# A Hymba layer on one Trainium2 core: the fourth pair's Gram blocks later, the second pair's norms later, a narrower first chunk

## The chip, the cores and the metric

One core of one Trainium2 chip runs the whole layer. The core has a matrix engine (TensorE, PE in the profile), VectorE (DVE), ScalarE (ACT), GpSimd (POOL), and SyncE (SP), which here issues most of the transfers. The metric is the device time of one execution in microseconds, lower being better.

## What is computed

The layer normalises 528 rows (16 learned tokens and 512 of the input) of 2048 features, projects them once, mixes them in two branches, and projects back. Group A is the RWKV-7 recurrence over 16 heads of 64; group B is a gated convolution of width 3.

```python
hn = _rmsnorm(h_res, norm_in_g[l])
P = hn @ w_in[l]
...
def step(S, inp):
    r_t, w_t, k_t, v_t, kk_t, b_t = inp
    sa = jnp.einsum('bhvk,bhk->bhv', S, kk_t)
    S = (S * w_t[:, :, None, :]
         - sa[..., None] * b_t[:, :, None, :]
         + v_t[..., None] * k_t[:, :, None, :])
    y_t = jnp.einsum('bhvk,bhk->bhv', S, r_t)
    return S, y_t
```

All arithmetic is float32. The output has 512 rows of 2048.

## The kernel before

**The flow.** The input projection runs as 65 column groups of 128 columns. Each float32 product is three matmuls: high half of the weights by high half of x, high by low, low by high (`steps`, L319 to L331, matmul L328). These matmuls are one long generator, here called the flow. A group is named after its columns: `ps_g` is a gate, `ps_r`, `ps_k`, `ps_v` are the operands of a head pair, `ps_B`, `ps_C`, `ps_h`, `ps_gc` belong to the convolution. A group takes two of the four accumulator banks of the pool `main`, so its first matmul must wait until whoever last used that bank has been read out.

**What stands between the flow.** All other matrix work is written by hand into the flow. `fill(ns)` lets the flow run for so many nanoseconds of planned time (0.43 ns for each moving column, so about 110 ns for 256 columns) and then returns to the code that called it; the table `FW` holds the lengths. `until(what, i)` runs the flow until a group is ready. `later(ns, fn)` issues a transfer when the flow has got so far. So a number in `FW` sets where on TensorE's queue a piece of other work stands. The order on TensorE is exactly that of the program; on the other engines a scheduler sets the order by priorities, and a block under `ahead()` is given a higher one.

**A head pair.** `prepare(i)` (L627 to L831) runs for eight pairs of heads, numbered 0 to 7. It builds decay factors (a scan into `cc`, L641), the left operand `ar`, and the right operand `bk` with three 64-column parts for each of nine chunks of 64 rows (DVE L649 and L660). ACT then copies between the two halves of the 128 partitions: L652 fills part 2 of the lower half, L661 part 2 of the upper half, L662 part 0 of the upper half. After a fill of `gram` or `gram_b` plus `shift` come the 36 Gram matmuls (L684): for each chunk and head one 64-row product of `bk` and `ar`. They write six tiles: `g_0` and `g_4` for chunks 0 to 7, and `g_8` for the last chunk, which takes two banks of `main`. DVE multiplies each by a mask into `gt` (L694); that read frees the banks. Then follow a fill of `gram2` minus `shift`, the norms (`n_misc`, `n_tz`, `zb`, L716 to L720), and on DVE two transposes of `bk` into `bt` (L730) and one of `v` into `vs` (L822). Because `shift` is added before the Gram blocks and taken off after them, a change of it moves the Gram blocks and leaves the norms where they were. Of the Gram matmuls only those of the upper half read a copied part, that of L661; what L652 and L662 write is read by L730 alone.

**Who else uses the engines.** ACT and either DVE or POOL split each new block of weights into its halves (tile `w`, L134 and L135). DVE also scales each finished group out of its banks (`pr_g`, `pr_v` and so on, L352).

**The recurrence.** `invert` solves the triangular systems of two pairs together and stores the results in a DRAM buffer `opd`. `recur` (L939 to L1025) then walks over nine chunks. `load_chunk` (L931 to L937) reads, for every pair, a slab of 128 partitions by 640 columns of `opd` into `ct`; SP issues these loads. Columns 0 to 127 of a slab hold `ar` (`O_AR`), the following ones the Gram blocks, the solved operands and `bt`. Chunk 0 starts from a zero state. So its first products `rz` (L958) are only those of the Gram part, and the products with `ar` (the branch `part == 0`, and L979 under `if c`) are left out. The recurrence begins after the fill `begin`, which follows the last `invert`.

Of the kernel before, what the change touches and what calls it, by code (L numbers as in the profile page):

```python
# [18 lines left out]
P = 128  # L19
# [6 lines left out]
NCH = SEQ // CH + 1  # L26
# [11 lines left out]
OPW = 10 * CH  # L38
O_AR, O_G, O_UV, O_B = 0, 128, 384, 512
# [2 lines left out]

FW = dict(
    evac=34, start=1062, lora=2200, gram=8000, gram_b=13500, gram2=5500, misc=2000, v=2000, vt=1000, solve=24500, solve_first=30000,
    tr=3200, lev=3000, cp=4200, out=1500, begin=20100, p=2900, u=2900, s=5200, last=3700, mix=2600,
)


# [29 lines left out]
def hymba_kernel(ctx: ExitStack, tc: tile.TileContext, xt, xtok, front, w_in, w_out, pv, lup, cst, msk, gf, out):  # L78
    nc = tc.nc
    ctx.enter_context(tc.manual_schedule(engines={mybir.EngineType.PE}))  # L80
    cp = ctx.enter_context(tc.tile_pool(name="cp", bufs=1))
# [12 lines left out]
    def col(off, i=0):  # L94
        return pvt[:, off + i : off + i + 1]
# [201 lines left out]
    with tc.issue_after(head):  # L297
        nc.vector.tensor_scalar(
            out=omm, in0=pvt[:, V_MU : V_MU + 33], scalar1=-1.0, scalar2=1.0, op0=ALU.mult, op1=ALU.add
        )  # L300
        for d, off in (
# [4 lines left out]
                out=d, in0=pvt[:, off : off + 8], scalar1=0.5, scalar2=None, op0=ALU.mult  # L306
            )
        nc.vector.tensor_scalar(
            out=hv[:, 4], in0=pvt[:, V_KA : V_KA + 8], scalar1=-0.5, scalar2=1.0, op0=ALU.mult, op1=ALU.add
# [232 lines left out]
    def step():  # L542
        t = next(flow, None)
        if t is None:
            run_pending(float("inf"))
        else:
            clock[0] += t
            run_pending(clock[0])
        return t

    def fill(ns):
        while ns > 0:
            seen = len(ready)
            t = step()
            if t is None:
                return
            ns -= t
            if len(ready) > seen:
                ns += FW["evac"]
# [26 lines left out]
    def c3(t):  # L586
        return t.rearrange("p (c s) -> p c s", s=CH)
# [10 lines left out]
    def split(t, name, n):  # L598
        hi = tr(f"{name}_h", F32R)[:, 0:n]
        lo = tr(f"{name}_l", F32R)[:, 0:n]  # L600
        nc.scalar.copy(hi, t)
        nc.vector.tensor_tensor(out=lo, in0=t, in1=hi.bitcast(F32), op=ALU.subtract)
        return hi, lo
# [6 lines left out]
    def spot(i, row, rows_n, c0, cn, step, o, n):  # L610
        d = opd[i]
        return bass.AP(
            tensor=d.tensor, offset=d.offset + (c0 * P + row) * OPW + o, ap=[[OPW, rows_n], [step * P * OPW, cn], [1, n]]
        )
# [12 lines left out]
    def prepare(i):  # L627
        p = i % 2
# [3 lines left out]
        bk = cq.tile([P, NCH, 3, CH], F32, tag="bk", name=f"bk{i}")  # L632
# [16 lines left out]
        nc.vector.scalar_tensor_tensor(  # L649
            out=bk[:, :, 1], in0=c3(k), scalar=hv[:, 2, i : i + 1], in1=c3(te), op0=ALU.mult, op1=ALU.mult  # L650
        )
        nc.scalar.copy(bk[0:64, 0 : NCH - 1, 2], bk[64:128, 0 : NCH - 1, 1])  # L652
        nc.gpsimd.tensor_scalar(
            out=ta, in0=ta, scalar1=hv[:, 3, i : i + 1], scalar2=hv[:, 4, i : i + 1], op0=ALU.mult, op1=ALU.add
        )
        nc.vector.scalar_tensor_tensor(
            out=ar[:, :, 0], in0=c3(k), scalar=col(V_KK, i), in1=e1[:, :, 0:CH], op0=ALU.mult, op1=ALU.mult
# [1 line left out]
        nc.vector.tensor_tensor(out=ta, in0=ta, in1=k, op=ALU.mult)  # L659
        nc.vector.tensor_tensor(out=bk[:, :, 0], in0=c3(ta), in1=c3(e2), op=ALU.mult)  # L660
        nc.scalar.copy(bk[64:128, :, 2], bk[64:128, :, 0])  # L661
        nc.scalar.copy(bk[64:128, 0 : NCH - 1, 0], bk[0:64, 0 : NCH - 1, 1])  # L662
        nc.gpsimd.tensor_copy(dd[:, :, place[i]], e1[:, :, CH])
        nc.gpsimd.memset(ar[:, 0, 1], 0.0)
        until("r", i)
# [2 lines left out]
            out=ar[:, 1:NCH, 1], in0=c3(r), in1=e1[:, 1:NCH, 1 : CH + 1], op=ALU.mult  # L668
        )
        nc.vector.scalar_tensor_tensor(  # L670
            out=r, in0=r, scalar=hv[:, 5, i : i + 1], in1=ta[:, CH:LP], op0=ALU.mult, op1=ALU.mult
# [3 lines left out]
        nc.scalar.activation(sq, k, AF.Square, scale=col(V_KK, i))  # L675
        sqh, sql = split(sq, f"sq{i}", LP)
        rh, rl = split(r, f"rk{i}", SEQ)
        shift = {0: 2000, 1: 2500, 3: -4000}.get(i, 0)
        fill(FW["gram_b" if p else "gram"] + shift)

        gt = cq.tile([P, 2, NCH, P], F32, tag=f"gt{p}", name=f"gt{i}")
# [9 lines left out]
        def masked(z, c0, c1):  # L691
            with ahead():
                for h in range(2):
                    nc.vector.tensor_tensor(  # L694
                        out=gt[:, h, c0:c1],
                        in0=z[h],
                        in1=gmask[:, h].unsqueeze(1).to_broadcast([P, c1 - c0, P]),
                        op=ALU.mult,
                    )
# [7 lines left out]
        masked(za, 0, 4)  # L707
        masked(zc, 4, 8)
        masked(ze, 8, 9)
        fill(FW["gram2"] - shift)  # L710

        n2 = tr(f"n2{i}")
        zn = [pool.tile([2, 288], F32, tag=t, name=f"n2_{i}_{t}") for pool, t in ((pi, "misc"), (pz, "tz"))]
# [12 lines left out]


        bt = cq.tile([P, NCH - 1, 2, CH // 2, 2], F32, tag="bt", name=f"bt{i}")
        for a in range(2):
            nc.vector.transpose(bt[:, :, :, :, a], bk[:, 0 : NCH - 1, 2 * a].rearrange("p c (t s) -> p c t s", t=2))  # L730

# [38 lines left out]
        for m in (2, 4, 8):  # L770
            for b in range(16 // (2 * m)):
# [4 lines left out]
                    out=pq,  # L776
# [5 lines left out]
                    out=tq.rearrange("p (i j) -> p i j", i=m), in_=pq, op=ALU.add, axis=AX.X  # L782
                )
                nc.vector.tensor_tensor(
                    out=pq,
# [143 lines left out]
        fill(FW["out"] if first < NPAIR - 2 else FW["begin"])  # L929

    def load_chunk(ch, c, pairs, ops):  # L931
        n = OPW if c < NCH - 1 else O_B
        if (c, 0) not in ops:
            for e in range(2):
                ops[c, e] = ch.tile([P, 4, OPW], F32, tag=f"ct{e}", name=f"ct{e}_{c}", bufs=2)
        for i in pairs:
            nc.sync.dma_start(ops[c, i % 2][:, i // 2, 0:n], spot(i, 0, P, c, 1, 1, 0, n))  # L937

    def recur(ch):  # L939
        ops = {}  # L940
        load_chunk(ch, 0, range(NPAIR), ops)
        load_chunk(ch, 1, range(NPAIR), ops)
        st = None
        pairs = [(k, e) for k in range(4) for e in range(2)]
        for c in range(NCH):
# [21 lines left out]
            if c and not last:  # L967
                load_chunk(ch, c + 1, range(4, NPAIR), ops)
# [93 lines left out]
    for i in range(0, NPAIR, 2):  # L1062
        invert([prepare(i), prepare(i + 1)])
# [9 lines left out]
    mix = [pp.tile([P, 4, SEQ], F32, tag=f"R{m}", name=f"mix{m}") for m in range(4)]  # L1073
# [256 lines left out]
    for half in range(2):  # L1330
        for g in range(4):
            b, m1, m2 = U[half, "P5", g], U[half, "M1", g], U[half, "M2", g]
# [194 lines left out]
```

## Time and profile before

| | us |
|---|---|
| median of three runs | 1004.63 |
| the three runs | 1006.38, 1004.63, 1003.05 |
| the profiled execution | 1005.19 |
| its span | 1003.4 |
| mean granted clock of TensorE | 0.997 |

The difference between the profiled execution's time and its span, 1.8 us, lies outside what the engines record. The page's lines give busy time by engine, chains of work and groups of instructions. A row of the timeline starts with the start in us and the duration in us; then come engine, line, operation and tiles, and, in brackets, how long the engine stood idle before it and for whom. Rows that follow one another with the same operation are put together ("x36"), so a row's duration then covers all of them. Ends of matmuls are modelled: two matmuls in sequence overlap, and the distance of two starts is a better measure than the duration.

### The profile page before, as it was taken

How to read it: one execution, taken by the hardware profiler on the slowest of the kernel's cores; microseconds unless marked ns; L12 is line 12 of the kernel's file. 1: busy time of each engine (PE TensorE's matmuls, PEld its weight loads, DVE VectorE, ACT ScalarE, POOL GpSimd, SP SyncE). 2: the span in 40 equal slices, each digit the busy share in tenths (PEclk: the TensorE clock that was granted, in tenths of full speed). 3: DMA queues.
4: the chain of work that ended last, by engine and by line, in shares of the span. 5: the costliest groups of instructions: out<-in, count | busy, mean ns of one | idle time of the engine just before them, and what ended most of it. 6: DMA issues, size and time to landing. Idle time of an engine off the chain costs nothing.

```text
span 1003.4 us, 22796 instructions
## 1 busy us (share of the span) xinstructions
PE 987.8 (98%) x9211; PEld 910.9 (91%) x9211; DVE 686.7 (68%) x1314; ACT 412.6 (41%) x770; POOL 266.9 (27%) x286
## 2 busy tenths in 40 slices
PE   9999999999999999999999999999999999999996
PEld 7999989999898999998999998889889898888885
DVE  6777966586765579745578745246554598999895
ACT  7554432354423435323434232232333325645553
POOL 0122323233223324232324222232323333001001
PEclk9999999999999999999999999999999999999998
DMA  9527484546673474954273954978784688798644
GB/s 324 156 79 182 113 227 105 149 135 161 152 203 97 123 189 94 240 142 111 91 204 98 235 138 109 342 270 276 227 251 136 168 256 227 241 290 224 140 103 167
DMA packets 184985, 180.00 MB, mean 179 GB/s; under 512 B 112176, under 2 KB 141616, under 8 KB 184368
## 3 DMA queue, kind: packets, MB, share of 16 engines
q1 hardware_dynamic: 182288, 169.64, 57.5%
q0 software_dynamic: 2304, 8.39, 4.8%
q8 instruction: 72, 1.18, 0.5%
q10 hardware_dynamic: 288, 0.52, 0.1%
q14 instruction: 33, 0.27, 0.1%
HBM read 139.80 MB, written 38.71 MB: 178 GB/s over the span
## 4 chain that ended last, share of the span: by engine, by line
PE 92%; DVE 3%; DMA 2%; issue 1%; ACT 1%; POOL 0%; DVEq 0%; SPq 0%; POOLq 0%
PE ps_r L328 9%; PE ps_h L328 9%; PE ps_B L328 9%; PE ps_gc L328 9%; PE ps_k L328 9%; PE ps_v L328 8%; PE ps_C L328 8%; PE M L1243 8%; PE ps_g L328 6%; PE P L1243 4%; PE Q L1243 2%; PE g L684 1%; DMA ct<-opd 1%; PE ps_lora L328 1%; PE rz L958 1%; PE zs L1005 1%
## 5 line engine op out<-in xcount | busy, mean ns | idle before, releaser
L135 POOL TENSOR_TENSOR w<-wr,w 128x512 fp32r<-128x512 f32 x119 | 169.1, 1421 | 371.7 <-ACT w L134 317.6
L134 ACT CAST w<-wr 128x512 fp32r<-128x512 f32 x252 | 153.6, 619 | 266.1 <-PE ps_k L328 44.3
L135 DVE TENSOR_TENSOR w<-wr,w 128x512 fp32r<-128x512 f32 x133 | 97.3, 736 | 107.8 <-ACT w L134 107.2
L328 PE MATMUL ps_k<-xh,w 128*128 128x256 f32 (+1 forms) x512 | 95.9, 285 | 0.2
L328 PE MATMUL ps_r<-xh,w 128*128 128x256 f32 (+1 forms) x512 | 95.2, 282 | 0.0
L328 PE MATMUL ps_v<-xh,w 128*128 128x272 f32 (+1 forms) x512 | 95.1, 283 | 0.0
L328 PE MATMUL ps_h<-xh,w 128*128 128x258 f32 (+1 forms) x512 | 93.2, 281 | 0.0
L328 PE MATMUL ps_C<-xh,w 128*128 128x258 f32 (+1 forms) x512 | 93.1, 281 | 0.0
L328 PE MATMUL ps_g<-xh,w 128*128 128x258 f32 (+1 forms) x512 | 91.6, 280 | 0.0
L328 PE MATMUL ps_B<-xh,w 128*128 128x512 f32 x256 | 83.6, 395 | 0.0
L328 PE MATMUL ps_gc<-xh,w 128*128 128x512 f32 x256 | 81.5, 392 | 0.0
L328 PEld LDWEIGHTS ps_k<-xh,w 128*128 128x128 f32 x512 | 80.1, 189 | 0.8 <-DVE w L135 0.3
L328 PEld LDWEIGHTS ps_r<-xh,w 128*128 128x128 f32 x512 | 80.3, 189 | 0.3
L328 PEld LDWEIGHTS ps_v<-xh,w 128*128 128x128 f32 x512 | 80.1, 189 | 0.3
L328 PEld LDWEIGHTS ps_C<-xh,w 128*128 128x128 f32 x512 | 79.5, 189 | 0.6
L328 PEld LDWEIGHTS ps_h<-xh,w 128*128 128x128 f32 x512 | 79.5, 189 | 0.4
L328 PEld LDWEIGHTS ps_g<-xh,w 128*128 128x128 f32 x512 | 79.2, 189 | 0.2
L328 PE MATMUL ps_k<-xl,w 128*128 128x256 f32 (+1 forms) x256 | 72.8, 284 | 0.0
L328 PE MATMUL ps_v<-xl,w 128*128 128x256 f32 (+1 forms) x256 | 72.5, 283 | 0.0
L328 PE MATMUL ps_g<-xl,w 128*128 128x256 f32 (+1 forms) x256 | 72.4, 283 | 0.0
L328 PE MATMUL ps_r<-xl,w 128*128 128x256 f32 (+1 forms) x256 | 72.2, 282 | 0.0
L328 PE MATMUL ps_h<-xl,w 128*128 128x256 f32 (+1 forms) x256 | 72.2, 282 | 0.0
(312 smaller groups left out, 2197.4 us busy)
## 6 DMA issues: line engine op xcount, KB each, us to landing
wr<-in_w_in_dram SPq DMA_DIRECT2D x126, 512.0 KB
ct<-opd SPq DMA_DIRECT2D x64, 320.0 KB
wo<-in_w_out_dram SPq DMA_DIRECT2D x21, 512.0 KB
opd<-gt SPq DMA_DIRECT2D x16, 576.0 KB
x<-in_w_out_dram POOLq DMA_DIRECT2D x16, 512.0 KB, 5.6
opd<-ar SPq DMA_DIRECT2D x8, 576.0 KB
opd<-bt SPq DMA_DIRECT2D x64, 64.0 KB
x<-in_w_out_dram SPq DMA_DIRECT2D x8, 512.0 KB
```

Source lines behind the costliest of these rows:

```text
L134: nc.scalar.copy(hi, rq)
L135: low[q] = eng.tensor_tensor(out=lo, in0=rq, in1=hi.bitcast(F32), op=ALU.subtract).ins
L328: nc.tensor.matmul(ps[r], ww[:, w], xx[:, kt, a:b], start=(kt == 0 and n == 0), stop=(kt == KT - 1 and n == 2))
L684: nc.tensor.matmul(z[h][:, c - c0], bk[hs, c, h : h + 2, :].rearrange("p a s -> p (a s)"), ar[hs, c].rearrange("p a s -> p (a s)"), start= ...
L958: nc.tensor.matmul(z[e][ho if e else hs, 0, k], ct[e][hs, k, o : o + CH], uv(e, k, hs, h) if part else st[hs, 4 * e + k], start=(part == 0 ...
L1005: nc.tensor.matmul(zs[hs, j], bb[:, h], uv(e, k, everything, h), start=True, stop=True)
L1243: nc.tensor.matmul(bank[s], left(prod, jj, m, s), w, start=(jj == 0 and n == 0), stop=(jj == 7 and n == 2))
```

## The change

Five edits. (1) The copies L652 and L662 stand later in the program text, after the norms and just ahead of the transposes that read them. Lines between L652 and L729 therefore have a number lower by one or two in the changed kernel (the Gram matmul is L682 there, the masks L692, the norms L714 to L718). (2) `load_chunk` reads for chunk 0 the columns from `O_G` on, which is 128, instead of from 0: 512 of 640 columns. (3) `begin` grows from 20100 to 20600. (4) `shift` of pair 3 goes from −4000 to −2000. (5) The fill between Gram blocks and norms of pair 1 grows by 700.

```diff
-    tr=3200, lev=3000, cp=4200, out=1500, begin=20100, p=2900, u=2900, s=5200, last=3700, mix=2600,
+    tr=3200, lev=3000, cp=4200, out=1500, begin=20600, p=2900, u=2900, s=5200, last=3700, mix=2600,
...
-        nc.scalar.copy(bk[0:64, 0 : NCH - 1, 2], bk[64:128, 0 : NCH - 1, 1])
...
-        nc.scalar.copy(bk[64:128, 0 : NCH - 1, 0], bk[0:64, 0 : NCH - 1, 1])
...
-        shift = {0: 2000, 1: 2500, 3: -4000}.get(i, 0)
+        shift = {0: 2000, 1: 2500, 3: -2000}.get(i, 0)
...
-        fill(FW["gram2"] - shift)
+        fill(FW["gram2"] - shift + 700 * (i == 1))
...
         bt = cq.tile([P, NCH - 1, 2, CH // 2, 2], F32, tag="bt", name=f"bt{i}")
+        nc.scalar.copy(bk[0:64, 0 : NCH - 1, 2], bk[64:128, 0 : NCH - 1, 1])
+        nc.scalar.copy(bk[64:128, 0 : NCH - 1, 0], bk[0:64, 0 : NCH - 1, 1])
...
-        n = OPW if c < NCH - 1 else O_B
+        a, b = 0 if c else O_G, OPW if c < NCH - 1 else O_B
...
-            nc.sync.dma_start(ops[c, i % 2][:, i // 2, 0:n], spot(i, 0, P, c, 1, 1, 0, n))
+            nc.sync.dma_start(ops[c, i % 2][:, i // 2, a:b], spot(i, 0, P, c, 1, 1, a, b - a))
```

On TensorE the same instructions run in both kernels. In pair 1 there are 34 matmuls of the flow between the Gram blocks and the norms, where there were 28. Everything of pairs 2 and 3 then stands 6 or 7 matmuls later in the flow. In pair 3 the Gram blocks stand after 80 matmuls of the group `ps_g`, where they stood after 55. The first products of the recurrence stand after 18 matmuls of the group `ps_h`, where they stood after 13.

Three places show how the instructions move. The first is the end of pair 3's Gram blocks, on TensorE and on DVE. On TensorE, 41 matmuls of the same group follow the last Gram matmul in the kernel before, and then the next group `ps_g` starts in new banks. In the changed kernel the last twelve rows up to that start are these (two matmuls, one row, stand between the last Gram matmul and the first row here; `ps_g_0_3377` and `ps_g_1_3378` are the old group's banks, `ps_g_0_3540` is the first one of the next group):

```order
L328 MATMUL ps_g_0_3377<-xl,w_3192 128x256
L328 MATMUL ps_g_0_3377<-xh,w_3192 128x256
L328 MATMUL ps_g_1_3378<-xh,w_3192 128x258
L328 MATMUL ps_g_1_3378<-xl,w_3192 128x258
L328 MATMUL ps_g_1_3378<-xh,w_3192 128x258 x2
L328 MATMUL ps_g_1_3378<-xl,w_3192 128x258
L328 MATMUL ps_g_1_3378<-xh,w_3192 128x258 x2
L328 MATMUL ps_g_1_3378<-xl,w_3192 128x258
L328 MATMUL ps_g_1_3378<-xh,w_3192 128x258 x2
L328 MATMUL ps_g_1_3378<-xl,w_3192 128x258
L328 MATMUL ps_g_1_3378<-xh,w_3192 128x258
L328 MATMUL ps_g_0_3540<-xh,w_3229 128x256
```

So 16 matmuls instead of 41 now stand between the Gram blocks and a group that starts in the bank of `g_8_0`.

On DVE, around the masks of the same pair, before:

```order
L730 STREAM_TRANSPOSE bt_3635<-bk_3138 128x512
L135 TENSOR_TENSOR w_3373<-wr_3371,w_3373 128x512
L363 SCALAR_TENSOR_TENSOR v_3359<-pr_v_3361,omm,sh_v_3367 128x16
L363 SCALAR_TENSOR_TENSOR v_3359<-pr_v_3361,omm,sh_v_3367 128x512
L730 STREAM_TRANSPOSE bt_3635<-bk_3138 128x512
L694 TENSOR_TENSOR gt_3450<-g_0_0_3451,cs 128x512
L694 TENSOR_TENSOR gt_3450<-g_0_1_3452,cs 128x512
L694 TENSOR_TENSOR gt_3450<-g_4_0_3453,cs 128x512
L694 TENSOR_TENSOR gt_3450<-g_8_0_3455,cs 128x128
L694 TENSOR_TENSOR gt_3450<-g_4_1_3454,cs 128x512
L694 TENSOR_TENSOR gt_3450<-g_8_1_3456,cs 128x128
L822 STREAM_TRANSPOSE vs_3707<-v_3359 128x576
```

The same place in the changed kernel:

```order
L730 STREAM_TRANSPOSE bt_3640<-bk_3145 128x512 x2
L135 TENSOR_TENSOR w_3371<-wr_3369,w_3371 128x512
L363 SCALAR_TENSOR_TENSOR v_3357<-pr_v_3359,omm,sh_v_3365 128x16
L363 SCALAR_TENSOR_TENSOR v_3357<-pr_v_3359,omm,sh_v_3365 128x512
L595 TENSOR_TENSOR lul_4455<-lur_4453,luh_4454 128x256
L135 TENSOR_TENSOR w_3407<-wr_3405,w_3407 128x512
L692 TENSOR_TENSOR gt_3474<-g_0_0_3475,cs 128x512
L692 TENSOR_TENSOR gt_3474<-g_0_1_3476,cs 128x512
L822 STREAM_TRANSPOSE vs_3714<-v_3357 128x576
L692 TENSOR_TENSOR gt_3474<-g_4_0_3477,cs 128x512
L692 TENSOR_TENSOR gt_3474<-g_8_0_3479,cs 128x128
```

One more split of weights (`w_3407`) stands ahead of the masks, the transpose `vs` stands in the middle of them, and a piece of the next pair's preparation (`lul`, L595) stands just ahead of them; the latter stood some 20 instructions earlier before.

The second place is SP's queue at the loads of chunk 0 (tiles `ct_0`). Before, and then in the changed kernel, up to the first load of chunk 1:

```order
L142 DMA wr_8281<-in_w_in_dram 128x1024
L937 DMA ct_0_8308<-opd_68 128x640
L451 DMA mixd_96<-cv_7887 128x512
L937 DMA ct_0_8309<-opd_69 128x640
L937 DMA ct_0_8308<-opd_70 128x640
```

```order
L142 DMA wr_8281<-in_w_in_dram 128x1024
L937 DMA ct_0_8313<-opd_68 128x512
L451 DMA mixd_96<-cv_7887 128x512
L937 DMA ct_0_8314<-opd_69 128x512
L937 DMA ct_0_8313<-opd_70 128x512
```

The order is the same and all eight loads of chunk 0 are narrower; those of chunk 1 behind them keep 640 columns. Further on, two loads of the later stage (`rb`, `gg`) stand ahead of the loads of chunk 2, where they stood behind them.

The third is DVE's queue in chunk 8, the last of the recurrence, where L988 copies what the products `zy` wait for. Before, and then in the changed kernel:

```order
L429 SCALAR_TENSOR_TENSOR cv_10292<-u_10040,pvt,cv_10292 128x512
L988 COPY ct_8_9849<-rz_0_10183 64x4x64 x2
L429 SCALAR_TENSOR_TENSOR cv_10292<-u_10040,pvt,cv_10292 128x512
L135 TENSOR_TENSOR w_10298<-wr_10296,w_10298 128x512
L1036 TENSOR_TENSOR ya_10283<-zy_10286,ya_10283 128x512
```

```order
L429 SCALAR_TENSOR_TENSOR cv_10252<-u_10040,pvt,cv_10252 128x512 x2
L988 COPY ct_8_9853<-rz_0_10187 64x4x64 x2
L135 TENSOR_TENSOR w_10258<-wr_10256,w_10258 128x512
L1036 TENSOR_TENSOR ya_10303<-zy_10306,ya_10303 128x512
L1037 TENSOR_REDUCE nv_10349<-ya_10303 128x8
```

Both convolution steps L429 now stand ahead of the two copies.

## The prediction

> **What bounds the kernel now.** I read the page first, for the engine that sets the end, and then the waits of that engine, since only time in which it stands idle can be won without taking work away. The rows of the page:
>
> ```profile
> span 1003.4 us, 22796 instructions
> PE 987.8 (98%) x9211; PEld 910.9 (91%) x9211; DVE 686.7 (68%) x1314; ACT 412.6 (41%) x770; POOL 266.9 (27%) x286
> PE 92%; DVE 3%; DMA 2%; issue 1%; ACT 1%; POOL 0%; DVEq 0%; SPq 0%; POOLq 0%
> ```
>
> TensorE is busy for 987.8 of 1003.4 us, so it stands idle for 15.6. The change removes no matmul; it can act through these 15.6 us, or make new ones. The view of TensorE's waits, and windows of 50 us (the first pair of numbers is the window's length and TensorE's busy time), say what they are and where:
>
> ```profile
> PE n_misc L716 <- DVE gt L694: 1.7, 1, 1.7
> PE rz L958 <- DMA ct<-opd: 1.4, 3, 0.5
> PE g L684 <- DVE pr_v L352: 1.1, 1, 1.1
> PE g L684 <- DVE bk L660: 0.6, 1, 0.6
> 100.00:150.00 50.00, 48.08 (x420) 47.14 (x419) 40.38 (x90) 19.57 (x36) 15.41 (x17) 1.00 0.67 169
> 250.00:300.00 50.00, 48.13 (x409) 46.77 (x408) 34.66 (x82) 15.89 (x28) 13.63 (x14) 1.00 0.67 171
> 600.00:650.00 50.00, 48.57 (x532) 43.36 (x522) 20.05 (x40) 13.65 (x26) 10.74 (x9) 1.00 0.67 219
> ```
>
> Three stages hold a gap each: 1.9 us near 130 us (norms of pair 1 wait for the masks), 1.9 us near 255 us (Gram blocks of pair 3 wait for `bk` and then for `pr_v`), 1.4 us near 636 us (the recurrence waits for its loads). The edits (5), (4) and (2) with (3) move just these three places. What is won there reaches the end only if TensorE doesn't wait again behind it; with 92% of the chain on TensorE, I take it that it arrives in full.
>
> **Edit (5), norms of pair 1 six matmuls later.** The timeline of that place:
>
> ```profile
> 125.46 0.38 PE L328 MATMUL ps_g<-xl,w 128*128 128x256 f32 x1
> 127.04 1.30 POOL L135 TENSOR_TENSOR w<-wr,w 128x512 fp32r<-128x512 f32 x1 [4.59 <-ACT w L134]
> 127.27 1.61 DVE L135 TENSOR_TENSOR w<-wr,w 128x512 fp32r<-128x512 f32 x1
> 128.74 0.28 PE L328 MATMUL ps_g<-xl,w 128*128 128x256 f32 x1
> 128.81 2.87 DVE L694 TENSOR_TENSOR gt<-g,cs 128x512 f32<-128x512 f32 x6
> 130.74 0.29 PE L716 MATMUL n_misc<-sq_h,ones 128*2 128x288 f32 x1 [1.72 <-DVE gt L694]
> ```
>
> The 28 matmuls from 125.46 to 128.74 start (128.74 − 125.46)/27 = 0.121 us apart. Six more fill 6 × 0.121 = 0.7 us of the 1.72 us in which TensorE waits for DVE. DVE's masks don't depend on these six, so they end when they did, and 1.0 us of wait stays: **−0.7**. Bounds: 0, if DVE comes later by as much; −0.7.
>
> The price is that pairs 2 and 3 stand six or seven matmuls later against groups that don't move. In pair 2 the group `ps_r` starts in the bank that the mask of `g_8` frees:
>
> ```profile
> 218.30 2.87 DVE L694 TENSOR_TENSOR gt<-g,cs 128x512 f32<-128x512 f32 x6
> 221.50 0.28 PE L328 MATMUL ps_r<-xh,w 128*128 128x256 f32 x1
> ```
>
> The fourth of the six masks is that of `g_8_0`; with four large and two small ones in 2.87 us, about 0.63 and 0.18, it ends at 218.30 + 3 × 0.63 + 0.18 = 220.4 (an estimate). That is 1.1 us ahead of `ps_r`. Seven matmuls less take 0.85 of it, and one split of weights that moves ahead of the masks takes some 0.65 more. So a wait of 0 to 0.5 us is born there; I count 0.3 for it inside the next step, where TensorE and DVE meet again.
>
> **Edit (4), Gram blocks of pair 3 twenty-five matmuls later.** TensorE and DVE there:
>
> ```profile
> 253.61 0.46 PE L684 MATMUL g<-ar,bk 64*128 64x128 f32 x2 [0.62 <-DVE bk L660]
> 254.22 2.06 PE L684 MATMUL g<-ar,bk 64*128 64x128 f32 x32 [0.15 <-ACT bk L661]
> 257.38 0.46 PE L684 MATMUL g<-ar,bk 64*128 64x128 f32 x2 [1.10 <-DVE pr_v L352]
> 257.76 0.39 PE L328 MATMUL ps_g<-xl,w 128*128 128x256 f32 x1
> 262.59 0.40 PE L328 MATMUL ps_g<-xh,w 128*128 128x258 f32 x2
> 239.93 1.36 DVE L641 TENSOR_TENSOR_SCAN cc<-smask,tz 128x576 f32<-128x576 f32 x1 [1.01 <-POOL tz L639]
> 259.78 2.84 DVE L694 TENSOR_TENSOR gt<-g,cs 128x512 f32<-128x512 f32 x6
> 262.54 0.76 DVE L822 STREAM_TRANSPOSE vs<-v 128x576 f32<-128x576 f32 x1
> 263.23 0.65 DVE L135 TENSOR_TENSOR w<-wr,w 128x512 fp32r<-128x512 f32 x1
> ```
>
> In pair 1 the 36 Gram matmuls ran unhindered (none of the waits above is theirs). Here the stage takes 257.76 − 253.61 + 0.62 = 4.8 us. Unhindered it would be the 2.06 us of 32 matmuls × 36/32 = 2.3 at most, so 2.5 to 2.6 us are lost; the waits give only 1.9, since the pipeline also drains and fills around each. 25 matmuls × 0.121 = 3.0 us put off the start by more than that, so `bk` and `pr_v` are ready and these waits go: −2.6 on their own.
>
> What is late next is the mask of `g_8_0`. Before, the next group starts with the second matmul of the row at 262.59, at 262.71, and the mask ended at about 259.78 + 3 × 0.62 + 0.18 = 261.8, so 0.9 us were to spare. Now 16 instead of 41 matmuls lie between. Without any wait that group would start at 262.71 − 2.6 − 0.7 + 0.3 = 259.7. When does DVE free the bank? Its queue from the scan `cc` to the first mask took 259.78 − 239.93 = 19.85 us, nearly all of it work in order, and the change adds one split of weights (0.65, the row at 263.23) to it, less some of the time in which it waited: 19.6 to 20.3. The transpose `vs` (0.76, some 0.7 of it not overlapped) now stands between the masks: three large masks, one small one and `vs` make 3 × 0.62 + 0.18 + 0.70 = 2.7. The bank is free 22.3 to 23.0 us after `cc` starts. `cc` itself moves forward with the flow, by 0.4, and by up to 1.0 more if POOL, for which it waited 1.01, is sooner done: 238.5 to 239.9. Free at 260.8 to 262.9, middle 261.7. This mask, not the flow, decides when the group starts: a new wait of about 2.0 us. Against 262.71 the whole of pairs 1 to 3 leaves **−1.0** (bounds −3.0, had the bank been free in time, and +0.2).
>
> The Trainium skill, in "SBUF — State Buffer", section "Who interferes with whom", says that a DVE operation with two inputs from SBUF can't run beside a GpSimd operation that reads SBUF, and that the later one is blocked for the whole of the other. The trace agrees: DVE's split at 127.27 began under POOL's and took 1.61 us, where the one at 263.23 took 0.65. By that rule the additional split could cost DVE 1.6 instead of 0.65, and the bank would come 1.0 us later; the sum would be −2.0 instead of −3.0.
>
> **Edit (1), the copies.** In the scheduled order ACT's copies keep their places in six of eight pairs and move a little in two, and no matmul waits on either in any pair. Cost **0**: ACT works 41% of the span, which hides 2 × 0.62 us per pair wherever they stand; uncovered, 1.2 us per pair only if the transposes `bt` were waited for, which the waits don't show.
>
> **Edits (2) and (3), the recurrence's start.** The first stage of chunk 0, the next stage of the same chunk for comparison, the loads in the chain of waits, and the DMA rate (the last number of the window, GB/s):
>
> ```profile
> 634.66 0.56 PE L958 MATMUL rz<-ct 64*64 64x64 f32 x20
> 637.32 0.33 PE L958 MATMUL rz<-ct 64*64 64x64 f32 x4 [0.51 <-DMA ct<-opd]
> 637.58 0.39 PE L328 MATMUL ps_h<-xl,w 128*128 128x258 f32 x1
> 640.98 0.69 PE L973 MATMUL rz<-pn,ct 64*64 64x64 f32 x32
> 641.60 0.39 PE L328 MATMUL ps_h<-xl,w 128*128 128x258 f32 x1
> 630.90 6.38 DMA ct<-opd
> 630.00:632.00 2.00, 2.00 (x19) 2.00 (x18) 0.83 (x2) 0.62 (x1) 0.00 (x0) 1.00 1.04 410
> ```
>
> The 32 matmuls of `rz` take 637.58 − 634.66 = 2.9 us, the 32 of the next stage 641.60 − 640.98 = 0.6: 2.3 are lost. The last four start at 637.32 where 635.2 would do, so the last load is 2.1 us late. The DMA engines are saturated at 410 GB/s, so bytes set the landings: eight loads lose 8 × 128 × 128 × 4 = 0.52 MB, which at 410 GB/s is 1.3 us. Five matmuls more of the flow (5 × 0.121) put the need 0.6 us later. Together 1.9 of 2.1; a wait of 0.2 stays: **−2.1**. Bounds: −2.3 (all gone), and −0.6 if a load costs the same whatever its width.
>
> The page "DMA: Bandwidth & Descriptors" of the Trainium skill, section "Bandwidth", speaks against narrower loads: it finds a higher rate for larger ones and asks for 1 MiB. No run here shows loads of two widths in this place; by its fixed part of 2.0 us ("Anatomy of one DMA — SWDGE (gpsimd) path") a load would be shortened by 5% rather than 20%.
>
> **Chunk 8.** The products `zy` wait for the copies L988:
>
> ```profile
> 776.70 1.01 DVE L429 SCALAR_TENSOR_TENSOR cv<-u,pvt,cv 128x512 f32<-128x512 f32 x1 [2.17 <-ACT cv L427]
> 777.74 0.88 DVE L988 COPY ct<-rz 64x256 f32<-64x256 f32 x2
> 778.54 0.73 DVE L429 SCALAR_TENSOR_TENSOR cv<-u,pvt,cv 128x512 f32<-128x512 f32 x1
> 778.41 1.29 PE L1009 MATMUL zy<-ct 128*64 128x64 f32 x32
> ```
>
> The second L429 now goes ahead and delays the copies by up to 0.73; TensorE, which had next to no margin (the first copy ends about 778.18, `zy` starts at 778.41), comes 0.6 later by edit (3). So 0 to 0.7; I take **+0.1**.
>
> **The sum.** −1.0 − 2.1 + 0.1 + 0 = −3.0 us. The profiled execution took 1005.19 (span 1003.4 and 1.8 around it) and becomes 1002.2; it lies 0.56 above the median, so on the scale of the median 1004.63 − 3.0 = 1001.6.
>
> **The rivals.**
> (a) The masks come in time. `cc` is at 238.5 and the queue short by a wait or two; the bank is free near 260 and the first three terms stand in full: −3.0 − 2.1 + 0.1 = −5.0, so 999.6. For it: 1.01 us of DVE's wait at `cc` can vanish. Against: even 238.5 + 22.3 is 260.8.
> (b) The new mask wait eats all of pairs 1 to 3. The bank comes at 262.7 or later, for instance with a split held up as at 127.27: 0 − 2.1 + 0.1 = −2.0, so 1002.6. For it: the row at 127.27. Against: POOL and DVE overlap only at some splits.
> (c) The loads don't shorten, since latency rather than bytes sets them (6.38 us of one load in the chain): −1.0 − 0.6 + 0.1 = −1.5, so 1003.1. Against: 410 GB/s.
> (d) Slower. The recurrence, five matmuls later in the flow, puts its copies behind the convolution's work on DVE not in chunk 8 alone but in all eight chunks from 1 on. Each time one or both of the L429 steps stand ahead, 0.73 to 1.74 us; at 0.9 that is 8 × 0.9 = +7.2, and with the other terms at −3.1 the kernel comes out +4.1, at 1008.7. It turns slower than before from 3.1/8 = 0.4 us a chunk, and by over 3.0 us from 0.8. For it: next to no margin in chunk 8. Against: in the order of instructions only chunk 8 shows such a swap.
>
> **How the numbers follow.** What a measurement of this kernel can tell from no change is about 0.3%, or 3.0 us. My forecast has a chance of 0.52; its own range is −4.3 to −1.7 and a little over half of it, 0.28, lies beyond −3.0. (a) has 0.26, as `cc` and the queue each have slack that I could only bound. (b) 0.06, (c) 0.05, (d) 0.11, with whatever else the scheduler's new order may cost. Faster: 0.28 + 0.26 = 0.54; within: 0.24 + 0.06 + 0.05 = 0.35; slower: 0.11. The range leaves out (d) and the far ends of (a): from 1004.63 − 6.0 = 998.6 to 1004.63 + 0.4 = 1005.0.
>
> **What would show it.** The wait of `n_misc` at pair 1 falls to 1.0; no wait of L682 in pair 3; a new wait of `ps_g` for DVE's masks near 259 to 262 us, about 2 us; `rz` of chunk 0 in 0.6 to 0.9 us, its loads landing some 0.66 us apart; at most 0.7 before `zy` in chunk 8. The prediction is wrong if that new wait is missing, if `rz` still takes over 2 us, or if a wait appears at a place not named here.

## The result, and the profile after

| | before | changed |
|---|---|---|
| median of seven runs, us | 1004.54 | 1009.02 |
| lowest and highest | 1003.05, 1006.38 | 1007.41, 1011.22 |
| profiled execution, its span | 1005.19, 1003.4 | 1007.93, 1006.1 |

The ratio of the changed kernel to the one before is 1.0045, with a 95% interval of 1.0031 to 1.0060: the change costs about 4.5 us. The forecast was a gain of 3.0. The two profiled executions differ by less, 1007.93 − 1005.19 = 2.7 us, since that of before lies 0.65 us above its kernel's median and that of the changed kernel 1.1 below. TensorE's waits in the changed kernel (total, times, longest, in us; the warm-up's 1.4 and 0.2 at `zb`, the same in both kernels, are left out):

```profile
PE ps_g L328 <- DVE gt L692: 5.5, 1, 5.5
PE n_misc L714 <- DVE gt L692: 1.0, 1, 1.0
PE ps_r L328 <- DVE gt L692: 0.4, 1, 0.4
PE g L682 <- DVE bk L659: 0.2, 1, 0.2
PE g L682 <- ACT bk L660: 0.2, 1, 0.2
```

Four of the five rows are what was forecast in kind and size: 1.0 us is left of the wait at the norms of pair 1, 0.4 is born in pair 2, the waits of the Gram blocks in pair 3 have nearly gone, and no wait of `rz` is left. The first row was forecast in kind, at 2.0 us. It is 5.5. Windows of five microseconds around it show a second loss (the third number from the right is the granted clock of TensorE):

```profile
255.00:260.00 5.00, 4.75 (x52) 4.24 (x52) 4.93 (x11) 4.00 (x8) 1.36 (x2) 1.00 0.52 123
260.00:265.00 5.00, 0.00 (x0) 0.00 (x0) 5.00 (x7) 0.61 (x1) 1.58 (x2) 0.71 0.79 212
265.00:270.00 5.00, 4.65 (x25) 4.65 (x26) 3.27 (x9) 1.35 (x2) 0.16 (x1) 0.61 0.77 156
270.00:275.00 5.00, 5.00 (x43) 4.74 (x41) 0.69 (x1) 2.35 (x5) 1.29 (x1) 1.00 0.00 0
```

TensorE does nothing from 260 to 265 us while DVE (the third busy time) works throughout. The clock falls, and it stays low after the work has come back: 0.71 and 0.61 in two windows are 2 × 5 × (0.29 + 0.39) = 6.8 us at half clock. The wait's other side is DVE's and POOL's timeline in the same kernel:

```profile
239.58 1.36 DVE L641 TENSOR_TENSOR_SCAN cc<-smask,tz 128x576 f32<-128x576 f32 x1 [0.62 <-POOL tz L639]
252.91 1.85 DVE L659 TENSOR_TENSOR bk<-ta,e 128x576 f32<-128x576 f32 x1
258.71 1.92 DVE L363 SCALAR_TENSOR_TENSOR v<-pr_v,omm,sh_v 128x16 f32<-128x16 f32 x2
260.89 1.75 DVE L135 TENSOR_TENSOR w<-wr,w 128x512 fp32r<-128x512 f32 x1
262.56 1.28 DVE L692 TENSOR_TENSOR gt<-g,cs 128x512 f32<-128x512 f32 x2
264.45 1.64 DVE L692 TENSOR_TENSOR gt<-g,cs 128x512 f32<-128x512 f32 x4
247.96 3.58 POOL L652 TENSOR_SCALAR ta<-ta,hv 128x576 f32<-128x576 f32 x1 [2.79 <-DVE te L648]
252.57 1.58 POOL L135 TENSOR_TENSOR w<-wr,w 128x512 fp32r<-128x512 f32 x1
258.64 1.30 POOL L135 TENSOR_TENSOR w<-wr,w 128x512 fp32r<-128x512 f32 x1 [4.49 <-ACT w L134]
260.69 1.40 POOL L135 TENSOR_TENSOR w<-wr,w 128x512 fp32r<-128x512 f32 x1 [0.51 <-ACT w L134]
265.35 0.58 PE L328 MATMUL ps_g<-xh,w 128*128 128x256 f32 x1 [5.45 <-DVE gt L692]
```

The same `bk` and `v`, and POOL's splits near them, in the kernel before:

```profile
252.72 0.75 DVE L660 TENSOR_TENSOR bk<-ta,e 128x576 f32<-128x576 f32 x1
258.35 0.88 DVE L363 SCALAR_TENSOR_TENSOR v<-pr_v,omm,sh_v 128x16 f32<-128x16 f32 x2
254.90 1.64 POOL L135 TENSOR_TENSOR w<-wr,w 128x512 fp32r<-128x512 f32 x1 [4.08 <-ACT w L134]
258.59 1.80 POOL L135 TENSOR_TENSOR w<-wr,w 128x512 fp32r<-128x512 f32 x1 [2.06 <-ACT w L134]
```

Three DVE operations take 1.75 to 1.92 us where their like took 0.75, 0.88 and 0.65 in the kernel before (the row of `v` covers two instructions each time). Each begins 0.07 to 0.34 us behind a split of weights on POOL. In the kernel before `v` overlaps with a split too, but there DVE began first, by 0.24 us: DVE took 0.88 us and POOL's split 1.80 instead of 1.30. So it matters here which of the two begins first. From the scan to the first mask it is 262.56 − 239.58 = 23.0 us instead of the 19.6 to 20.3 forecast. The scan itself starts at 239.58, which is 240.1 on the time scale of the profile before (the changed kernel's profile runs 0.5 us early, see below): 0.2 us behind the forecast range of 238.5 to 239.9.

Where did the time go? Both kernels run the flow's matmuls in the same order, so the start of the same matmul can be compared in the two traces. The table is worked out from these starts, with the difference set to zero at 60 us (the two executions began 0.5 us apart).

| behind | changed minus before, us | step |
|---|---|---|
| norms of pair 1 (140) | −0.8 | −0.8 |
| solve of pairs 0 and 1 (190) | −1.4 | −0.6 |
| masks of pair 2 (229) | −0.7 | +0.7 |
| masks of pair 3 (275) | +4.9 | +5.6 |
| solve of pairs 2 and 3 (340) | +4.8 | −0.1 |
| start of the recurrence (645) | +2.75 | −2.1 |
| chunk 8 (800) | +3.1 | +0.3 |

Pair 1 and the recurrence stand as forecast, the first solve is better by 0.6 us, and pair 2 (+0.7 for 0.3) and chunk 8 (+0.3 for +0.1) are a little worse. Pair 3 is the loss.

### The profile page after: what moved, and what is told of

Its sections match the earlier page's. It is cut to its first block, busy times and chain, and to the rows that moved or that the text cites. A ratio compares the mean times of both kernels' runs of the same rounds, so it can differ in the third digit from the quotient of the medians.

```text
span 1006.1 us, 22797 instructions
## 1 busy us (share of the span) xinstructions
PE 989.1 (98%) x9211; PEld 912.4 (91%) x9211; DVE 688.9 (68%) x1314; ACT 412.1 (41%) x770; POOL 268.9 (27%) x286
## 4 chain that ended last, share of the span: by engine, by line
PE 88%; DVE 6%; POOL 2%; issue 2%; DMA 1%; ACT 1%; DVEq 0%; SPq 0%; POOLq 0%; ACTq 0%
PE ps_C L328 9%; PE ps_gc L328 9%; PE ps_h L328 9%; PE ps_B L328 8%; PE ps_k L328 8%; PE ps_r L328 8%; PE M L1243 8%; PE ps_v L328 7%; PE ps_g L328 6%; PE P L1243 4%; PE Q L1243 2%; PE ps_lora L328 1%; PE g L682 1%; PE zs L1005 1%; PE rz L958 1%
## 5 line engine op out<-in xcount | busy, mean ns | idle before, releaser
L328 PE MATMUL ps_C<-xl,w 128*128 128x256 f32 (+1 forms) x256 | 72.5, 283 | 0.0
```

The source lines that it names most:

```text
L328: nc.tensor.matmul(ps[r], ww[:, w], xx[:, kt, a:b], start=(kt == 0 and n == 0), stop=(kt == KT - 1 and n == 2))
```

## The experiments

Each kernel was timed in five rounds beside the kernel before. E2 to E4 and E7 to E8, and E10 to E12, start from the kernel before; E1, E5, E6 and E9 from the changed kernel. The medians of the kernel before, timed beside them, are 1004.32 us for e1 to e4, 1004.42 for e5 to e8 and 1004.68 for e9 to e12; the ratio is not the quotient of the medians.

| run | median, us | ratio to before (95%) |
|---|---|---|
| e1 changed, without edit 4 | 1006.11 | 1.0018 (1.0009 to 1.0027) |
| e2 edit 4 alone | 1006.31 | 1.0023 (1.0010 to 1.0035) |
| e3 edits 2 and 3 alone | 1002.98 | 0.9994 (0.9985 to 1.0004) |
| e4 edit 5 alone | 1006.94 | 1.0032 (1.0021 to 1.0044) |
| e5 changed, three splits off POOL | 1007.25 | 1.0030 (1.0019 to 1.0041) |
| e6 changed, masks of `g_8` first | 1008.30 | 1.0038 (1.0023 to 1.0052) |
| e7 edits 2, 3, and 5 taken back | 1001.21 | 0.9977 (0.9965 to 0.9990) |
| e8 as e7, shift −3400 | 1001.52 | 0.9973 (0.9962 to 0.9983) |
| e9 changed, three other splits off POOL | 1006.36 | 1.0020 (1.0009 to 1.0031) |
| e10 edit 1 alone | 1004.64 | 1.0002 (0.9993 to 1.0011) |
| e11 edit 2 alone | 1002.45 | 0.9986 (0.9976 to 0.9996) |
| e12 as e7, with 1500 | 1001.58 | 0.9969 (0.9956 to 0.9983) |

### Which edit loses: e1 to e4

E1 puts one number back:

```diff
-        shift = {0: 2000, 1: 2500, 3: -2000}.get(i, 0)
+        shift = {0: 2000, 1: 2500, 3: -4000}.get(i, 0)
```

> The changed kernel with the shift of pair 3 back at -4000 (edits 1, 2, 3 and 5 stay). Theory A (the loss is edit 4's: the next group waits for the mask of g_8_0 at the end of a long DVE queue, and the idle time slows TensorE's clock): the wait of 5.5 us for the masks near 260 us is gone, the two waits of before for bk and pr_v are back (about 1.9 us), the clock stays at 1.00; against before: pair 1 -0.7, solve of pairs 0 and 1 -0.6, pair 2 +0.7, recurrence -2.2, chunk 8 +0.3, sum -2.5, ratio about 0.9975. Theory B (the loss is made by edit 5, which puts pairs 2 and 3 six or seven matmuls later): a wait for the masks of 3 us or more stays, ratio 1.002 or more.

Neither theory holds. The wait for the masks is gone, yet the kernel is slower than before. Its longest waits at 1.0 us and more behind the start, and the window of five microseconds in which the first of them ends (the third number from the right is the granted clock):

```profile
PE g L682 <- DVE bk L659: 2.9, 1, 2.9
PE n_misc L714 <- DVE gt L692: 1.0, 1, 1.0
...
255.00:260.00 5.00, 3.83 (x34) 3.67 (x35) 4.93 (x11) 3.67 (x6) 0.51 (x2) 0.66 0.53 123
```

The Gram blocks wait 2.9 us for `bk`, where they waited 0.6 before, and the clock is at half speed for 3.4 us of that window, 0.66 on average. So edit 5 does harm, as theory B had it, but at `bk` and not at the masks.

E2 is that line alone on the kernel before:

```diff
-        shift = {0: 2000, 1: 2500, 3: -4000}.get(i, 0)
+        shift = {0: 2000, 1: 2500, 3: -2000}.get(i, 0)
```

> The kernel before with the shift of pair 3 at -2000 and nothing else (edit 4 alone). Theory A: the next group waits 3 to 5.5 us for the mask of g_8_0, the granted clock falls to about 0.5 for some us, the waits for bk and pr_v are gone; +2.5 to +6 us against before, ratio 1.0025 to 1.006. Theory B: no wait of over 1 us, -2.6 to 0 us, ratio 0.9974 to 1.000.

```profile
PE ps_g L328 <- DVE gt L694: 1.8, 1, 1.8
PE rz L958 <- DMA ct<-opd: 1.0, 2, 0.5
```

Edit 4 alone moves the wait to the masks, as theory A said, with a period of half clock behind it. The wait is 1.8 us, not 3 to 5.5, and the ratio, 1.0023, lies just below the range given. Compared matmul by matmul, pair 3 comes 1.0 us later than in the profile of before. From `cc` to the first mask it is 258.49 − 237.52 = 21.0 us here: the 19.85 of before and the added split of weights, which took 1.15 us beside POOL.

E3 takes edits 2 and 3 alone:

```diff
-    ... begin=20100, ...
+    ... begin=20600, ...
...
-        n = OPW if c < NCH - 1 else O_B
+        a, b = 0 if c else O_G, OPW if c < NCH - 1 else O_B
```

> The kernel before with edits 2 and 3 alone (chunk 0 loads 512 of 640 columns, begin 20600). Both theories: no wait of rz for its loads, the 32 matmuls of rz in 0.6 to 0.9 us, -2.2 us, ratio about 0.9978. A third one (a later recurrence loses on DVE in every chunk) expects new waits in the chunks and a ratio of 1.000 or more.

The stage does what was expected; these are the 32 matmuls of `rz` in one piece:

```profile
634.81 0.82 PE L958 MATMUL rz<-ct 64*64 64x64 f32 x32
```

Compared matmul by matmul, the flow gains 2.2 us there against the profile of before. The ratio, 0.9994, shows less than the −2.2 us, and its interval doesn't reach 0.9978. In this profile the unchanged wait of 1.7 us at pair 1 is followed by half clock, which it is not in the profile of before:

```profile
130.00:132.00 2.00, 1.22 (x6) 0.74 (x7) 2.00 (x5) 0.68 (x2) 0.00 (x0) 1.00 0.04 8
132.00:134.00 2.00, 2.00 (x12) 1.99 (x11) 1.24 (x3) 0.59 (x1) 0.14 (x1) 0.57 0.36 78
134.00:136.00 2.00, 2.00 (x12) 2.00 (x12) 0.49 (x2) 1.13 (x2) 0.44 (x1) 0.57 0.74 128
136.00:138.00 2.00, 2.00 (x19) 2.00 (x18) 0.00 (x0) 0.11 (x1) 0.85 (x1) 1.00 0.83 209
```

That cost 1.5 us of this execution. The runs that were only timed have no trace, but their mean granted clock is on record, and it doesn't order e3's times (1004.02 us at 0.998, 1002.36 at 0.995), so half clock alone doesn't explain them. The medians, 1002.98 beside 1004.32, show a gain of 1.3 us. The gap between −2.2 and the ratio stays open.

E4 takes edit 5 alone.

```diff
-        fill(FW["gram2"] - shift)
+        fill(FW["gram2"] - shift + 700 * (i == 1))
```

> The kernel before with edit 5 alone (norms of pair 1 six matmuls later). Theory A: the wait of n_misc falls from 1.7 to 1.0 us, a wait of ps_r for the masks of pair 2 of about 0.4 us is born, and pair 3 keeps its waits; -1.3 to 0 us, ratio 0.9987 to 1.000. Theory B: the next group of pair 3 waits for the masks by 2 us or more, ratio 1.002 or more.

Slower by 0.3%, through a wait that neither theory named: `bk` in pair 3.

```profile
247.10 1.06 DVE L775 TENSOR_TENSOR prod<-d,y 72x512 f32<-72x512 f32 x1
248.08 0.75 DVE L648 SCALAR_TENSOR_TENSOR te<-ta,e 128x576 f32<-128x576 f32 x1
248.93 3.58 POOL L653 TENSOR_SCALAR ta<-ta,hv 128x576 f32<-128x576 f32 x1 [2.79 <-DVE te L648]
253.54 1.55 POOL L135 TENSOR_TENSOR w<-wr,w 128x512 fp32r<-128x512 f32 x1
253.89 1.82 DVE L660 TENSOR_TENSOR bk<-ta,e 128x576 f32<-128x576 f32 x1
255.85 0.46 PE L684 MATMUL g<-ar,bk 64*128 64x128 f32 x2 [2.32 <-DVE bk L660]
```

In the kernel before:

```profile
246.56 0.74 DVE L648 SCALAR_TENSOR_TENSOR te<-ta,e 128x576 f32<-128x576 f32 x1
248.08 1.05 DVE L775 TENSOR_TENSOR prod<-d,y 72x512 f32<-72x512 f32 x1
247.40 2.36 POOL L653 TENSOR_SCALAR ta<-ta,hv 128x576 f32<-128x576 f32 x1 [1.23 <-DVE te L648]
```

There `te` (L648) came ahead of the 512-wide step of another pair's solve (L775); now it comes behind it. `te` releases POOL's L653, which takes 3.58 us instead of 2.36. DVE's two-input operations beside it are the likely reason, but no run takes them away. POOL's next split starts 0.35 us ahead of `bk`, and `bk` takes 1.82 us. From the start of `cc` (240.55) to the start of `bk` it is 13.3 us here and 12.8 in e2, e3, e7 and the kernel before.

### What makes the mask late: e5, e6 and e9

E5 leaves out what POOL reads in three blocks (`q` counts half blocks of weights); the low halves of these weights are zero.

```diff
+        if q in (83, 85, 87):
+            low[q] = eng.memset(lo.bitcast(F32), 0.0).ins
+        else:
             low[q] = eng.tensor_tensor(out=lo, in0=rq, in1=hi.bitcast(F32), op=ALU.subtract).ins
```

> The changed kernel, with the low half of three blocks of weights left out: GpSimd's three splits of weights that run near 253, 259 and 261 us are replaced by a memset of zeros, which writes but reads nothing. The order on VectorE is the same as in the changed kernel. Theory C (the masks are late because VectorE's operations with two inputs in SBUF stand still while GpSimd's split reads SBUF): bk L659, v L363 and w L135 fall from 1.85, 1.92 and 1.75 us to about 0.75, 0.9 and 0.65, the wait for the masks from 5.5 to 2.3 to 3 us, the half clock lasts for one period of 3.4 us or none; 3 to 5 us less than the changed kernel, so ratio 0.9995 to 1.0015 against before. Theory D (VectorE's queue is simply too long; GpSimd has no part in it): those three keep their durations, the wait stays above 5 us, ratio 1.003 to 1.006.

The three blocks were those beside `v` and `w` and a later one; the split beside `bk` was still there and serves as a control. DVE in this kernel, and the memset beside `w`:

```profile
253.80 1.84 DVE L662 TENSOR_TENSOR bk<-ta,e 128x576 f32<-128x576 f32 x1
259.59 0.89 DVE L366 SCALAR_TENSOR_TENSOR v<-pr_v,omm,sh_v 128x16 f32<-128x16 f32 x2
260.73 0.69 DVE L138 TENSOR_TENSOR w<-wr,w 128x512 fp32r<-128x512 f32 x1
260.89 0.53 POOL L136 MEMSET w<- 128x512 f32 x1 [0.28 <-PE ps_g L331]
```

The two operations without a reading neighbour on POOL fall from 1.92 to 0.89 and from 1.75 to 0.69 us; the one whose neighbour stayed keeps 1.84. So theory C holds for the durations. The wait falls to 3.4 us, not to 2.3 to 3, the half clock still lasts two periods instead of one or none, and the ratio, 1.0030, misses the 0.9995 to 1.0015 expected. E9 replaces the three that stand beside `bk`, `v` and `w`:

```diff
-        if q in (83, 85, 87):
+        if q in (81, 83, 85):
```

> As e5, but with the memset in the place of those three splits of GpSimd that stood beside bk L659, v L363 and w L135 in the changed kernel (in e5 the one beside bk was still there and the third replaced one came later). The low halves of three blocks of weights are left out. Theory C: bk L659 now takes 0.75 instead of 1.85 us too, and the time from the scan cc to the first mask falls from 23.0 to about 19.8 us; the wait of the next group falls from 3.4 us in e5 to 2.0 to 2.6, with one period of half clock or none; ratio 1.000 to 1.002. Theory D: cc to the first mask stays above 21 us, ratio 1.003 or more.

```profile
239.65 1.36 DVE L644 TENSOR_TENSOR_SCAN cc<-smask,tz 128x576 f32<-128x576 f32 x1 [0.62 <-POOL tz L642]
253.00 0.75 DVE L662 TENSOR_TENSOR bk<-ta,e 128x576 f32<-128x576 f32 x1
252.61 1.00 POOL L136 MEMSET w<- 128x512 f32 x2
259.44 1.29 DVE L695 TENSOR_TENSOR gt<-g,cs 128x512 f32<-128x512 f32 x2
```

Beside a memset `bk` is back at 0.75, and `cc` to the first mask at 259.44 − 239.65 = 19.8 us, which was the forecast. So the 3.2 us by which DVE's queue was longer than forecast are the three collisions. A wait of 3.1 us stays all the same, above the 2.0 to 2.6 expected, because the flow, not held up at `bk`, wants the bank sooner. Even without collisions edits 4 and 5 together lose.

E6 puts the masks of `g_8` first:

```diff
-        masked(za, 0, 4)
-        masked(zc, 4, 8)
-        masked(ze, 8, 9)
+        if i == 3:
+            first = masked(ze, 8, 9)
+            with tc.issue_after(first):
+                masked(za, 0, 4)
+                masked(zc, 4, 8)
+        else:
+            masked(za, 0, 4)
+            masked(zc, 4, 8)
+            masked(ze, 8, 9)
```

> The changed kernel with the two masks of g_8 ahead of the other four in pair 3. All theories in which the next group waits for the mask of g_8_0 and nothing else: the wait falls from 5.5 by two large masks, to 3.3 to 3.8 us, and with it the half clock from two periods of 3.4 us to one; 1.9 to 3.6 us less than the changed kernel, ratio 1.001 to 1.0026 against before. If the group waits for something else, the ratio stays at 1.0045.

The wait falls to 3.7 us and the half clock to one period, as expected; in the profile the stage loses 1.9 us less than in the changed kernel. The ratio, 1.0038, lies above the 1.001 to 1.0026 expected and is not told apart from 1.0045.

### Edit 5 without its side effect: e7, e8 and e12

E7 takes the 700 off again in the next fill of the same pair, so that pair 2 and all behind it stand where they stood; edits 2 and 3 are in.

```diff
-        fill(FW["gram2"] - shift)
+        fill(FW["gram2"] - shift + 700 * (i == 1))
...
-        fill(FW["misc"])
+        fill(FW["misc"] - 700 * (i == 1))
```

> The kernel before with edits 2 and 3, and with edit 5 whose 700 is taken off again from the next fill of the same pair, so that pairs 2 and 3 stay where they were. Theory E (edit 5 loses because it moves pairs 2 and 3, which changes VectorE's order there): the wait of n_misc falls to 1.0 us, no wait in pair 2, pair 3 waits as before (about 1.9 us in all, no more), rz without waits; -0.7 - 2.2 = -2.9 us, ratio about 0.9971. If the later norms themselves do harm, the ratio is 1.000 or more.

Faster than before, at 0.9977. Around pair 3 DVE runs its instructions in the same order as in e3, and no wait for `bk` exists:

```profile
PE n_misc L716 <- DVE gt L694: 1.0, 1, 1.0
PE g L684 <- DVE pr_v L352: 0.6, 1, 0.6
```

So the later norms do no harm. What they push along with them does.

E8 is e7 with

```diff
-        shift = {0: 2000, 1: 2500, 3: -4000}.get(i, 0)
+        shift = {0: 2000, 1: 2500, 3: -3400}.get(i, 0)
```

> As e7, and the shift of pair 3 at -3400, half a microsecond later than before. Theory E with the mask queue as the next limit: the wait for bk (0.6 us) is gone, that for pr_v halves, the next group comes 0 to 1 us earlier until it meets the mask of g_8_0; -2.7 to -3.9 us, ratio 0.9961 to 0.9973. If any move of the Gram blocks loses, the ratio is above that of e7.

With the Gram blocks half a microsecond later, the wait for `pr_v` is gone and 0.2 us of the mask's wait appear: the two limits lie that close together. The ratio, 0.9973, is not told apart from e7's.

E12 is e7 with

```diff
-        fill(FW["gram2"] - shift + 700 * (i == 1))
+        fill(FW["gram2"] - shift + 1500 * (i == 1))
...
-        fill(FW["misc"] - 700 * (i == 1))
+        fill(FW["misc"] - 1500 * (i == 1))
```

> As e7 with 1500 instead of 700 (norms of pair 1 thirteen or fourteen matmuls later, taken back in the next fill of the pair). If the masks' end decides when the norms run: the wait of n_misc falls from 1.0 to 0.2 us or less and the rest stays; e7 less 0.8 us, ratio 0.9965 to 0.997. If the solve behind the norms becomes late: a new wait near 165 to 180 us or an order on VectorE as in e4, ratio above 0.998.

```profile
PE pwarm L187 <- DVE cold L184: 1.4, 1, 1.4
PE g L684 <- DVE pr_v L352: 0.7, 1, 0.7
PE zb L719 <- ACT n L723: 0.2, 1, 0.2
```

No wait is left at pair 1, and no new one appears: behind TensorE's warm-up (`pwarm`) that for `pr_v` in pair 3, 0.7 us, is the only one above 0.2. 0.9969 is the lowest ratio of all, though its interval overlaps with those of e7 and e8. All three are faster than both kernels.

### Edits 1 and 2 alone: e10 and e11

E10 moves the two copies as the change does; e11 takes the lines of `load_chunk`, with `begin` at 20100.

```diff
-        nc.scalar.copy(bk[0:64, 0 : NCH - 1, 2], bk[64:128, 0 : NCH - 1, 1])
...
-        nc.scalar.copy(bk[64:128, 0 : NCH - 1, 0], bk[0:64, 0 : NCH - 1, 1])
...
         bt = cq.tile([P, NCH - 1, 2, CH // 2, 2], F32, tag="bt", name=f"bt{i}")
+        nc.scalar.copy(bk[0:64, 0 : NCH - 1, 2], bk[64:128, 0 : NCH - 1, 1])
+        nc.scalar.copy(bk[64:128, 0 : NCH - 1, 0], bk[0:64, 0 : NCH - 1, 1])
```

> The kernel before with edit 1 alone (the copies later in the text). Prediction: cost 0, ratio 0.999 to 1.001, no new wait of TensorE. A rival: the new order of pairs 2 and 3 on VectorE and ScalarE, not the six matmuls, makes bk late; then the wait for bk in pair 3 is above 2 us and the ratio 1.002 or more.

1.0002 (0.9993 to 1.0011), and no new wait: edit 1 costs nothing and brings nothing.

> The kernel before with edit 2 alone (512 of 640 columns in chunk 0, begin at 20100). By bytes: the last load comes 1.3 us earlier, a lateness of 0.8 us stays of 2.1, rz in about 1.4 us instead of 2.9; -1.3 us, ratio about 0.9987. By a fixed cost for each load: rz stays at 2.5 to 2.9 us, ratio 1.000.

```profile
632.75 0.85 PE L958 MATMUL rz<-ct 64*64 64x64 f32 x28
633.94 0.33 PE L958 MATMUL rz<-ct 64*64 64x64 f32 x4 [0.35 <-DMA ct<-opd]
```

One wait of 0.35 us is left for the last load, where three made 1.4 us. The flow gains 1.5 us there and the kernel 0.9986, against −1.3 and 0.9987 expected. So the narrower load does most of the work, by its bytes, and `begin` the remainder.

## Why the prediction was wrong

**The recurrence's start: right.** −2.1 was forecast, −2.1 measured, with the split between bytes and later start confirmed by e11.

**Edit 1: right,** by e10.

**Pair 1, pair 2 and chunk 8: right in the trace, to 0.4 us.** −0.8 for −0.7 at pair 1; a wait of 0.4 for 0.3 in pair 2, which comes 0.7 later with it; and +0.3 for +0.1 in chunk 8. The 0.6 us gained in the first solve were not forecast.

**Pair 3: the step that failed.** The step read: DVE's "queue from the scan `cc` to the first mask took 259.78 − 239.93 = 19.85 us, nearly all of it work in order, and the change adds one split of weights". The mechanism was the right one. The term was mis-sized at three points.

First, 19.6 to 20.3 us became 23.0. The durations were carried over from a profile in which the same operations met POOL's splits at other moments. The neighbours on POOL make 0.75, 0.88 and 0.65 us into 1.85, 1.92 and 1.75. Rival (b) had this mechanism with one held-up split at 1.0 us, and a chance of 0.06; there were three, and e5 and e9 show them to be the whole of the difference. Two of them struck operations that were in the queue before, `bk` and `v`; the prediction asked for a collision only at the split that was added.

Second, a wait was priced at its own length. It costs more: 6.8 us at half clock followed, and the matmuls behind it, 3.5 us of them from 265.35 on, took twice their time, which is about 1.7 us. E2 shows it without edit 5: the wait there is 1.8 us, close to the 2.0 forecast, and pair 3 still comes out 1.0 us later, not earlier.

Third, edit 5 was priced by the matmuls it moves, with pairs 2 and 3 as a matter of 0.3 us. E4 and e7 show what that left out: six matmuls' shift turned the order of `te` and the solve on DVE, and with it came the collision that makes `bk` late. The forecast followed the changed order at the masks only, not at the operations ahead of them.

Pairs 1 to 3 were to bring −1.0 us and cost +4.9. The wait, longer by 5.5 − 2.0 = 3.5, and the 1.7 at half clock are 5.2 of these 5.9 us.

One number of the sum was a single sample. The 2.6 us that the Gram blocks of pair 3 lost in the profile of before are 1.6 us less in e3, e7 and e10 and 1.5 less in e11, where pair 3 stands as in the kernel before: only `pr_v`, 0.6 to 0.7 us, is waited for there. So edit 4 had about 1 us to win, not 2.6.

Rival (d), the slower one, named the wrong place: chunk 8 took 0.3 us, and the seven chunks ahead of it next to nothing. Its 1008.7 us lie close to the measured 1009.0 by luck.

## What to carry to other kernels

A shift in a hand-ordered queue should be taken back before the next stage, or it moves that stage against every queue ordered by a scheduler. When a duration is carried over from one profile to another order, ask which neighbour on POOL it will meet, and which of the two begins first; here that made 0.65 to 0.88 into 1.75 to 1.92 us three times over. And price a stall of the matrix engine together with the slow clock that may follow, since a stall removed at one place and made a little longer at another is no even exchange.

## What the runs showed of the hardware

**Collisions of DVE with POOL.** DVE operations that read two operands from SBUF waited out POOL's split when it had begun first: 1.92 and 0.89, 1.75 and 0.69, 1.84 and 0.75 us for the same instruction with and without it. A POOL operation that only writes didn't delay them: a memset ran beside `w` in e5 and beside `bk` in e9. In e9 nothing of POOL was left beside `v`. The rule of the Trainium skill in "SBUF — State Buffer", section "Who interferes with whom", says just this, and e5 and e9 agree.

**The half clock.** Stalls of TensorE and the half clock behind them, from the waits and the windows of the fourteen profiles:

| stall, us | half clock behind it |
|---|---|
| 0.6 to 1.0 in one piece (pair 1 with edit 5, `pr_v` in e3, e7, e10, e11, e12) | none |
| 1.0 to 1.4 in two or three pieces (`rz`) | none in the profile of before; one period in e2, e4, e10 |
| 1.9 in three pieces (pair 3 of before) | none |
| 1.6 to 1.7 (pair 1) | none in before, e2, e10 and e11; one period in e3 |
| 1.8 to 3.1 (pair 3: e2, e4, e1, e9) | one period each |
| 3.4 and 5.5 (e5, changed kernel) | two periods |
| 3.7 (e6) | one period |

A period is 3.4 us, e3's windows above: 2 × 2 × (0.43 + 0.43) = 3.4. It costs 1.7 us of the work that falls into it.

The clock records of the traces say more on when. Counted from the clock's first rise in each profile, every fall lies a whole number of 3.413 us later: (132.29 − 6.00)/3.413 = 37.0 in e3, (262.06 − 6.06)/3.413 = 75.0 in the changed kernel. So the falls keep to a fixed raster, and how much of a stall lies in one window of it goes with what follows (idle is the window less TensorE's busy time, with modelled ends):

| window that holds most of the stall | TensorE idle in it, us | clock in the next |
|---|---|---|
| pair 1, before, e10, e11 | 1.72, 1.55, 1.56 | full |
| pair 1, e2, the stall cut in two | 0.73 and 1.17 | full |
| pair 1, e3 | 1.88 | half |
| pair 3, e2 | 1.81 | half |
| pair 3, changed kernel, e1, e4, e5, e6, e9 | 2.16 to 2.86 | half |
| `rz`, before | 1.00 | full |
| `rz`, e2, e10, e4 | 1.12, 1.34, 1.37 | half |

Among the flow's matmuls the clock fell after windows with 1.8 us or more of idle time and stayed after 1.7 or less; around `rz`, with its small matmuls, 1.1 us were enough. Where the windows lie differs between executions, so the same stall of 1.7 us is followed by half clock in e3 and not in the others. E5's 3.4 us reached 1.0 us into a second window, and two periods followed; e6's 3.7 us lay 0.9 in one window and 2.7 in the next, and one followed. All this is read from fourteen profiles; no run moved a window.

One period lowers the mean granted clock of an execution by 1.7/1003 = 0.0017, and that is on record for every timed run. For the kernel before it accounts for part of the spread: of the 28 runs beside e9 to e12, the nine from 1002.5 to 1003.4 us have 0.997 to 0.999, and four of the five above 1005.9 have 0.994. For e7 and e12 it does not: e12's runs lie at 999.5 to 1000.8 and again at 1002.4 to 1003.2, both at 0.997 to 0.998. What parts these two groups stays open.

The Trainium skill, "TensorE: Matmul & The Clock Gate", section "Part 1: The HAM clock gate (the "warmup" mystery)", puts the window at 3413 ns and has it run freely, which agrees with the period and with the chance in it. It has the clock fall after an idle window; here it fell after windows that were idle for half of their time.
